# Two output units of mixer A in static weight slots, and a later attention and gated recurrence in the second layer

## The chip, the cores and the metric

The kernel runs on one core of a Trainium2 chip. TensorE (PE) does the matrix products, VectorE (DVE) and ScalarE (ACT) the elementwise work, SyncE (SP) issues most of the transfers and GpSimd (POOL) a few. The metric is the device time of one execution in microseconds (us), as the median of several runs.

## The reference

The reference is one inference step of a two-layer backbone on 128 context tokens and 256 latent tokens of width 1024. In each layer the normed tokens are scaled and shifted by a modulation, multiplied by one input projection, and go through four mixers side by side: A, a bidirectional RWKV-7 recurrence; B, a neighbourhood attention; C, a gated recurrence (HGRN2); D, a windowed attention with grouped heads. Their outputs, 256 columns each, are put side by side and multiplied by an output projection. Then a norm and a gate follow, the result is added to the residual, and a squared-ReLU MLP with 4096 hidden units does the same. In short:

```python
p = h @ w_in                                   # h = norm(x) * (1 + scale) + shift
y = concat([rwkv7(p), nat(p), hgrn2(p), swa(p)], -1) @ w_out
x = x + gate * rms(y)
h = rms(x) * (1 + scale2) + shift2
x = x + gate2 * rms(square(relu(h @ w1)) @ w2)
```

All is float32. Every float32 product is made of three products of a cheaper type, as the next section says.

## The kernel before

**Three products for one.** A float32 operand is split into a rounded big half and a remainder. A weight block of 128 x 1024, called a unit, arrives by a transfer in a slot `ws` (line 370), ACT casts its big half into `wh` (line 330), and DVE subtracts to make the remainder `wl` (line 318). The activations are split the same way into `hh` and `hl`. TensorE then adds wh x hh, wh x hl and wl x hh (line 333). An input unit is 24 matmuls of 384 columns, and a unit of the output projection is 18 matmuls of 512 columns.

**Slots.** The static slots live through the whole program: three `ws`, two `wh`, two `wl`. While the mixers run, all units use these. When a layer's mixers are done, `open_dense` opens further slots, `dws`, `dwh` and `dwl`, in memory that the mixers used. They are free only when the last reader of that memory is done. From then on `slot` (line 353) deals out static and dense slots in turns.

**Stages of a layer.** `rwkv_in` makes the first nine input units, which belong to mixer A. Then `merge` (line 1590) writes the four mixers interleaved: each has a clock that starts at an offset and runs at a rate, and the one whose clock is lowest is written next. The names ending in 1 are the second layer's: `ao1` is the offset of the neighbourhood attention, `ho1` that of the gated recurrence, `so1` that of the windowed attention, and `ul1` says how many steps the second half of mixer A stays behind the first. Mixer A's longest part is a chain: products, an inverse that goes through memory outside the core (transfers on SP at lines 957, 961, 973 and 977 with DVE work between them), then a set of 32 x 32 and 64 x 64 products, and `rwkv_post`, a norm on ACT and DVE that writes the two halves of mixer A's output into `hh` and `hl`.

**The end of a layer's mixing.** `wout_early` multiplies the six output units that belong to the mixers B, D and C. `wout` multiplies the two that belong to mixer A, units 0 and 1: unit 0 whole, unit 1 a 128-token tile at a time. Each tile then goes through `postnorm` (two squares with a sum on ACT, line 327; the root by a logarithm and an exponential; a scaled sum on DVE, lines 321 and 318, into the residual `x`) and `prenorm` (a square of `x`, the root, a scaling into `tmp`, line 324; eight transposes on TensorE, line 336; scale and shift; the split into `hh` and `hl`). The MLP begins with the first two units of w1, which wait for `hh`.

**What sets the order.** The program is written in the order that `merge` gives, but a scheduler then orders the instructions of each engine by a model of their durations. An engine runs its instructions in that order, and one that waits holds up all behind it. The model's price of a matmul pass is its columns by the clock and a constant gap.

Of the kernel before, what the change touches and what calls it, by code (L numbers as in the profile page):

```python
# [9 lines left out]

# [158 lines left out]
MIX = (5120, 12544, 15584)  # L169


P = {'hp': (0, 400), 'np': 3, 'we': 1, 'dp': [], 'ka': 0, 'pw': '', 'na': 2, 'nb': 2, 'pe': 'VAVA', 'xw': 4, 'wt': 4, 'xs': 2, 'mr': 2.5, 'ps': 7.4, 'po': 16, 'rw': (1.4, 1.4), 'ao': (80, 100), 'ar': (1.7, 1.4), 'so': (120, 120), 'sr': (1.4, 1.7), 'ho': (0, 0), 'hr': (0.8, 0.9), 'hl': (4, 4), 'lv': (2.0, 2.0), 'ul': (1, 1), 'rw0': 1.4, 'ao0': 80, 'ar0': 1.7, 'so0': 100, 'sr0': 1.4, 'ho0': 0, 'hr0': 0.9, 'hl0': 6, 'lv0': 4.0, 'ul0': 2, 'rw1': 1.4, 'ao1': 100, 'ar1': 1.7, 'so1': 120, 'sr1': 1.7, 'ho1': 0, 'hr1': 0.9, 'hl1': 4, 'lv1': 2.0, 'ul1': 3}
# [109 lines left out]
class Builder:  # L282
# [158 lines left out]
    def open_dense(self):  # L441
# [8 lines left out]
        for n, k, order in (("ws", self.xs, (0, 1)), ("wh", self.xw, (0, 1, 1)), ("wl", self.xw, (0, 1, 1))):  # L450
            q = self.pool("d" + n, k)
            self.wsets[n] = [((p[n], n), (q, "d" + n))[o] for o in order]
# [1179 lines left out]
    def dense_end(self, units, nxt, save, ahead=()):  # L1632
# [5 lines left out]
        for t in range(3):  # L1638
            for i, (src, y) in enumerate(units):
                self.rows_product(self.acc, *y, w[i], False, i == len(units) - 1, (t,))  # L1640
            self.postnorm(t, self.x[t], self.acc[t], self.gate)
            if save is not None:
                (self.nc.sync if save is self.io["y"] else self.nc.scalar).dma_start(save[t * 128:t * 128 + 128], self.x[t])
            if nxt is not None:
                self.prenorm(t, self.x[t], self.mods[nxt[0], nxt[1] + 1], self.mods[nxt[0], nxt[1]], self.h)
            yield len(units) * 1.3

# [4 lines left out]
    def mix(self, l, extra=()):  # L1652
# [15 lines left out]
        self.merge((0, p("rw"), self.rwkv(l), p("hp")), (p("ao"), p("ar"), attend(0), 0), (p("so"), p("sr"), attend(1), 0), (p("ho"), p("hr"), gated(), 0), *extra, then=self.wout_early(l))  # L1668
        self.open_dense()
# [16 lines left out]
    def wout(self, l):  # L1686
        s, y = self.wout_unit(l, 0)
        self.rows_product(self.acc, *y, self.unit(s), False, False)
        yield 3.9
        yield from self.dense_end([self.wout_unit(l, 1)], (l, 3), None, [self.io["w1"][l, n] for n in range(P["na"])])  # L1690
# [73 lines left out]
def program(layers=L, dbg=None):  # L1764
# [4 lines left out]
    for n, s in OUTS.items():  # L1769
        io[n] = nc.dram_tensor(n, s, F32, kind="ExternalOutput").ap()  # L1770
# [22 lines left out]
```

## Time and profile before

| What | us |
|---|---|
| median of 3 runs | 1402.37 |
| the runs | 1394.47, 1402.37, 1402.92 |
| profiled execution | 1390.85 |
| its span in the trace | 1389.1 |
| TensorE busy in the span | 1265.2 |

The profiled execution is 11.52 us shorter than the median. The span is cut into stages by the rows of the timeline: 0 to 60 is the start and the first modulation, 60 to 391 the first layer's mixers, 391 to 423 the end of its mixing, 423 to 742 its MLP, up to 752 the turn to the second layer, 752 to 1068 its mixers, 1068 to 1101 the end of its mixing, and 1101 to 1380 its MLP. A row of the timeline gives the start, the duration, the engine, the line, the operation and how many instructions it stands for; a bracket behind it gives the idle time of the engine just before it, and what ended that.

### The profile page before, as it was taken

Reading aid. Unit: us, or ns where it says so; the run is one execution under the profiler, and the core shown is the slowest. Engines: PE = TensorE matmul, PEld = TensorE weight load, DVE = VectorE, ACT = ScalarE, POOL = GpSimd, SP = SyncE. Lnnn points to the kernel's source line nnn. Section 1 sums busy time; section 2 is a strip of 40 time slices with the busy share of each in tenths; the row PEclk is TensorE's granted clock in tenths of the full one; section 3 lists DMA queues with packets and bytes.
Section 4 is the critical chain, followed back from the end, with each engine's and each line's share of the span. In section 5 each row is a group of like instructions: output and inputs, shape, how many; then the busy total and the mean of one; then the engine's idle time right before and its main releaser. Section 6 shows DMA issues by size and latency. Waiting matters only on the chain.

```text
span 1389.1 us, 20850 instructions
## 1 busy us (share of the span) xinstructions
PE 1265.2 (91%) x8174; PEld 1065.9 (77%) x8174; DVE 785.1 (57%) x1509; ACT 639.2 (46%) x1255; POOL 89.6 (6%) x165
## 2 busy tenths in 40 slices
PE   6899899899848999999997999899999499999997
PEld 2888788357738888878886888789776488999996
DVE  2598969644364444644544368987654633444442
ACT  4567533353254443534435578334544633333431
POOL 0000000000010212221000000100000000000000
PEclk8999899999986999999998999899999799999999
DMA  9332221761461888999852655136205454434411
GB/s 359 129 112 81 65 71 54 243 211 49 154 250 51 276 333 306 338 324 347 280 159 78 215 182 182 62 99 189 61 17 192 187 167 137 137 122 128 130 46 46
DMA packets 86899, 227.96 MB, mean 164 GB/s; under 512 B 24657, under 2 KB 27025, under 8 KB 86801
## 3 DMA queue, kind: packets, MB, share of 16 engines
q1 hardware_dynamic: 63040, 166.23, 36.8%
q0 software_dynamic: 12368, 44.60, 8.4%
q10 hardware_dynamic: 11392, 15.80, 3.6%
q8 instruction: 64, 1.05, 0.3%
q14 instruction: 35, 0.28, 0.1%
HBM read 205.33 MB, written 21.27 MB: 163 GB/s over the span
## 4 chain that ended last, share of the span: by engine, by line
PE 49%; DVE 9%; issue 6%; DMA 5%; ACT 4%; POOL 1%; SPq 0%; DVEq 0%; ACTq 0%; POOLq 0%
PE pd L333 24%; PE pr L333 12%; PE pm L333 11%; DVE mix L318 4%; DMA low<-wl 2%; ACT tmp L327 2%; DMA ws<-w 2%; ACT mix L327 1%; PE pm L336 1%; DVE tmp L321 1%; DVE wl L318 1%; DMA wl<-low 1%; DMA dws<-w 1%; ACT wh L330 1%; PE pd L336 1%
## 5 line engine op out<-in xcount | busy, mean ns | idle before, releaser
L333 PE MATMUL pd<-hh,wh 128*128 128x384 f32 (+2 forms) x640 | 221.6, 347 | 16.1 <-ACT hh L330 7.5
L333 PE MATMUL pd<-hh,wl 128*128 128x384 f32 (+2 forms) x640 | 221.3, 346 | 3.8 <-DVE wl L318 2.2
L333 PE MATMUL pd<-hl,wh 128*128 128x384 f32 (+2 forms) x640 | 218.6, 342 | 0.4 <-DVE hl L318 0.4
L330 ACT CAST wh<-ws 128x1024 fp32r<-128x1024 f32 x120 | 125.5, 1048 | 161.5 <-PE pd L333 67.8
L318 DVE TENSOR_TENSOR wl<-ws,wh 128x1024 fp32r<-128x1024 f32 x91 | 111.3, 1223 | 99.8 <-ACT wh L330 54.6
L318 DVE TENSOR_TENSOR mix<-mix 128x384 f32<-128x384 f32 (+19 forms) x288 | 134.6, 483 | 45.2 <-ACT mix L330 22.5
L333 PEld LDWEIGHTS pd<-hh,wh 128*128 128x128 f32 x640 | 124.4, 195 | 24.8 <-ACT hh L330 8.2
L333 PE MATMUL pd<-hh,dwh 128*128 128x384 f32 (+2 forms) x384 | 130.0, 341 | 8.4 <-ACT hh L330 6.7
L333 PEld LDWEIGHTS pd<-hh,wl 128*128 128x128 f32 x640 | 124.2, 194 | 10.4 <-issue 3.8
L333 PE MATMUL pd<-hl,dwh 128*128 128x384 f32 (+2 forms) x384 | 130.7, 341 | 0.7 <-DVE hl L318 0.6
L333 PE MATMUL pd<-hh,dwl 128*128 128x384 f32 (+2 forms) x384 | 130.2, 339 | 0.0
L333 PEld LDWEIGHTS pd<-hl,wh 128*128 128x128 f32 x640 | 124.6, 195 | 2.1 <-DVE hl L318 1.1
L327 ACT ACTIVATE mix<-mix 128x384 f32<-128x384 f32 (+4 forms) x188 | 106.9, 600 | 26.4 <-DVE mix L318 12.9
L333 PE MATMUL pr<-mix,mix 128*64 128x64 f32 (+3 forms) x1024 | 88.3, 238 | 9.3 <-DVE mix L318 6.3
L318 DVE TENSOR_TENSOR dwl<-ws,dwh 128x1024 fp32r<-128x1024 f32 x43 | 52.5, 1224 | 68.7 <-ACT dwh L330 67.2
L318 DVE TENSOR_TENSOR dwl<-dws,dwh 128x1024 fp32r<-128x1024 f32 x43 | 52.6, 1224 | 67.5 <-ACT dwh L330 67.5
L333 PEld LDWEIGHTS pr<-mix,mix 128*64 128x64 f32 (+3 forms) x1024 | 74.2, 149 | 20.3 <-issue 8.8
L333 PE MATMUL pm<-mix 128*32 128x32 f32 (+7 forms) x840 | 84.6, 271 | 2.1 <-DVE mix L318 1.3
L333 PEld LDWEIGHTS pd<-hh,dwh 128*128 128x128 f32 x384 | 75.5, 198 | 11.7 <-ACT hh L330 7.8
L333 PEld LDWEIGHTS pd<-hl,dwh 128*128 128x128 f32 x384 | 76.1, 198 | 2.9 <-DVE hl L318 1.5
L333 PE MATMUL pr<-dwh,f 128*128 128x512 f32 x240 | 77.2, 397 | 0.0
L330 ACT COPY mix<-pr 64x128 f32<-64x128 f32 (+7 forms) x136 | 42.2, 336 | 75.0 <-PE pr L333 45.4
(223 smaller groups left out, 2234.2 us busy)
## 6 DMA issues: line engine op xcount, KB each, us to landing
ws<-win SPq DMA_DIRECT2D x87, 512.0 KB, 4.5
ws<-w SPq DMA_DIRECT2D x64, 512.0 KB, 3.8
dws<-w SPq DMA_DIRECT2D x64, 512.0 KB, 5.2
wm<-modw POOLq DMA_DIRECT2D x56, 512.0 KB, 9.0
low<-wl POOLq DMA_DIRECT2D x29, 512.0 KB, 7.2
wl<-low SPq DMA_DIRECT2D x29, 512.0 KB, 3.8
ws<-modw SPq DMA_DIRECT2D x28, 512.0 KB, 4.8
ws<-wout SPq DMA_DIRECT2D x14, 512.0 KB, 4.6
```

The source lines that it names most:

```text
L318: (eng or self.nc.vector).tensor_tensor(out, a, b, op=op)
L321: self.nc.vector.scalar_tensor_tensor(out, a, s, b, op0=op0, op1=op1)
L327: self.nc.scalar.activation(out, a, fn, **kw)
L330: self.nc.scalar.copy(out, a)
L333: self.nc.tensor.matmul(out, l, r, start=start, stop=stop)
L336: self.nc.tensor.transpose(out, a, self.ident[:k, :k])
```

## The change

The static slots `wh` and `wl` become three each, and the dense slots `dwh` and `dwl` three each in place of four; `dws` is opened by another number (`xs`) and stays. The turns go dense, static, dense, static. At the end of `mix`, before the dense slots are opened, units 0 and 1 of the output projection are fetched and split in static slots (`self.last`), and `wout` uses them; the part of `dense_end` that norms one tile is a function of its own, `tile_end`. In the second layer the neighbourhood attention starts at clock 150 in place of 100, the gated recurrence at 40 in place of 0, and the second half of mixer A is two steps behind in place of three. The scheduler's gap for a matmul pass is set to 13 ns.

```diff
--- before.py
+++ after.py
@@ -7,6 +7,7 @@
 import concourse.tile as tile
 from concourse import mybir
 from concourse.bass_utils import run_bass_kernel_spmd
+from concourse.hw_specs import TRN2Spec
 
 F32 = mybir.dt.float32
 F32R = mybir.dt.float32r
@@ -166,10 +167,10 @@
 }
 
 
-MIX = (5120, 12544, 15584)
-
-
-P = {'hp': (0, 400), 'np': 3, 'we': 1, 'dp': [], 'ka': 0, 'pw': '', 'na': 2, 'nb': 2, 'pe': 'VAVA', 'xw': 4, 'wt': 4, 'xs': 2, 'mr': 2.5, 'ps': 7.4, 'po': 16, 'rw': (1.4, 1.4), 'ao': (80, 100), 'ar': (1.7, 1.4), 'so': (120, 120), 'sr': (1.4, 1.7), 'ho': (0, 0), 'hr': (0.8, 0.9), 'hl': (4, 4), 'lv': (2.0, 2.0), 'ul': (1, 1), 'rw0': 1.4, 'ao0': 80, 'ar0': 1.7, 'so0': 100, 'sr0': 1.4, 'ho0': 0, 'hr0': 0.9, 'hl0': 6, 'lv0': 4.0, 'ul0': 2, 'rw1': 1.4, 'ao1': 100, 'ar1': 1.7, 'so1': 120, 'sr1': 1.7, 'ho1': 0, 'hr1': 0.9, 'hl1': 4, 'lv1': 2.0, 'ul1': 3}
+MIX = (5120, 12544, 15488)
+
+
+P = {'hp': (0, 400), 'np': 3, 'we': 1, 'dp': [], 'ka': 0, 'pw': '', 'na': 2, 'nb': 2, 'pe': 'VAVA', 'xw': 3, 'wt': 4, 'xs': 2, 'mr': 2.5, 'ps': 7.4, 'po': 16, 'rw': (1.4, 1.4), 'ao': (80, 100), 'ar': (1.7, 1.4), 'so': (120, 120), 'sr': (1.4, 1.7), 'ho': (0, 0), 'hr': (0.8, 0.9), 'hl': (4, 4), 'lv': (2.0, 2.0), 'ul': (1, 1), 'rw0': 1.4, 'ao0': 80, 'ar0': 1.7, 'so0': 100, 'sr0': 1.4, 'ho0': 0, 'hr0': 0.9, 'hl0': 6, 'lv0': 4.0, 'ul0': 2, 'rw1': 1.4, 'ao1': 150, 'ar1': 1.7, 'so1': 120, 'sr1': 1.7, 'ho1': 40, 'hr1': 0.9, 'hl1': 4, 'lv1': 2.0, 'ul1': 2}
 
 
 def par(name, l):
@@ -447,7 +448,7 @@
         self.tmp = self.arena([a.tile([128, n], F32, name="tmp")], [n]).get
         self.wmod = self.pool("wm", 4)
         p = self.pools
-        for n, k, order in (("ws", self.xs, (0, 1)), ("wh", self.xw, (0, 1, 1)), ("wl", self.xw, (0, 1, 1))):
+        for n, k, order in (("ws", self.xs, (0, 1)), ("wh", self.xw, (1, 0)), ("wl", self.xw, (1, 0))):
             q = self.pool("d" + n, k)
             self.wsets[n] = [((p[n], n), (q, "d" + n))[o] for o in order]
 
@@ -1638,12 +1639,16 @@
         for t in range(3):
             for i, (src, y) in enumerate(units):
                 self.rows_product(self.acc, *y, w[i], False, i == len(units) - 1, (t,))
-            self.postnorm(t, self.x[t], self.acc[t], self.gate)
-            if save is not None:
-                (self.nc.sync if save is self.io["y"] else self.nc.scalar).dma_start(save[t * 128:t * 128 + 128], self.x[t])
-            if nxt is not None:
-                self.prenorm(t, self.x[t], self.mods[nxt[0], nxt[1] + 1], self.mods[nxt[0], nxt[1]], self.h)
+            self.tile_end(t, nxt, save)
             yield len(units) * 1.3
+
+    def tile_end(self, t, nxt, save):
+
+        self.postnorm(t, self.x[t], self.acc[t], self.gate)
+        if save is not None:
+            (self.nc.sync if save is self.io["y"] else self.nc.scalar).dma_start(save[t * 128:t * 128 + 128], self.x[t])
+        if nxt is not None:
+            self.prenorm(t, self.x[t], self.mods[nxt[0], nxt[1] + 1], self.mods[nxt[0], nxt[1]], self.h)
 
     def load_x(self):
         for t in range(3):
@@ -1666,6 +1671,7 @@
         self.run(self.rwkv_in(l, h))
         p = lambda n: par(n, l)
         self.merge((0, p("rw"), self.rwkv(l), p("hp")), (p("ao"), p("ar"), attend(0), 0), (p("so"), p("sr"), attend(1), 0), (p("ho"), p("hr"), gated(), 0), *extra, then=self.wout_early(l))
+        self.last = [self.unit(self.wout_unit(l, n)[0]) for n in (0, 1)]
         self.open_dense()
 
     def wout_unit(self, l, n):
@@ -1684,10 +1690,13 @@
             yield 3.9 * P["we"]
 
     def wout(self, l):
-        s, y = self.wout_unit(l, 0)
-        self.rows_product(self.acc, *y, self.unit(s), False, False)
-        yield 3.9
-        yield from self.dense_end([self.wout_unit(l, 1)], (l, 3), None, [self.io["w1"][l, n] for n in range(P["na"])])
+        units = [self.wout_unit(l, n) for n in (0, 1)]
+        self.prepare([self.io["w1"][l, n] for n in range(P["na"])])
+        self.rows_product(self.acc, *units[0][1], self.last[0], False, False)
+        for t in range(3):
+            self.rows_product(self.acc, *units[1][1], self.last[1], False, True, (t,))
+            self.tile_end(t, (l, 3), None)
+            yield 1.3
 
     def ffn(self, l, layers, halves):
         nc, io, h = self.nc, self.io, self.h
@@ -1768,11 +1777,12 @@
         io[n] = nc.dram_tensor(n, s, F32, kind="ExternalInput").ap()
     for n, s in OUTS.items():
         io[n] = nc.dram_tensor(n, s, F32, kind="ExternalOutput").ap()
+    TRN2Spec.PE_FULL_CLOCK_PASS_GAP_NS = 13.0
     with tile.TileContext(nc, schedule_with_timeline_sim=True) as tc:
         with ExitStack() as es:
             pool = lambda n, b, **kw: es.enter_context(tc.tile_pool(name=n, bufs=b, **kw))
             pools = {
-                "c1": pool("c1", 1), "ws": pool("ws", 3), "wh": pool("wh", 2), "wl": pool("wl", 2),
+                "c1": pool("c1", 1), "ws": pool("ws", 3), "wh": pool("wh", 3), "wl": pool("wl", 3),
                 "h": pool("h", 1), "prm": pool("prm", 1), "mt": pool("mt", 1),
                 "pm": pool("pm", 6 - P["np"], space=PSUM), "pr": pool("pr", P["np"], space=PSUM), "pd": pool("pd", 2, space=PSUM),
                 "dram": pool("dram", 2, space=DRAM), "spl": pool("spl", 1, space=DRAM),
```

The next rows are those of ACT at the end of the first layer's mixing. `mix_340` holds mixer A's values there, and the row with `eps` that reads `pr` is the logarithm in `rwkv_post`, once for each half of mixer A's output. Before:

```order
L327 ACTIVATE mix_340<-pr,eps 128x384
L327 ACTIVATE mix_340<-mix_340 128x384 x2
L327 ACTIVATE mix_340<-pr,eps 128x384
L330 CAST hh<-mix_340 128x384
L327 ACTIVATE mix_340<-mix_340 128x384
L519 DMA lora<-lora 128x768
L517 DMA prm<-prm 128x46
L330 CAST hh<-mix_340 128x384
L330 CAST dwh<-dws 128x1024 x2
L330 CAST dwh<-ws 128x1024 x2
L330 CAST wh<-dws 128x1024
L330 CAST dwh<-dws 128x1024
```

And now:

```order
L331 CAST dwh<-ws 128x1024 x2
L328 ACTIVATE mix_340<-mix_340 128x384
L331 CAST wh<-dws 128x1024
L328 ACTIVATE mix_340<-pr,eps 128x384
L328 ACTIVATE mix_340<-mix_340 128x384 x2
L331 CAST hh<-mix_340 128x384
L331 CAST dwh<-ws 128x1024
L328 ACTIVATE mix_340<-pr,eps 128x384
L520 DMA lora<-lora 128x768
L328 ACTIVATE mix_340<-mix_340 128x384
L518 DMA prm<-prm 128x46
L331 CAST hh<-mix_340 128x384
```

Four casts of the coming MLP's weights now stand ahead of the second half's logarithm, one of them from a dense slot; before, all casts of weights stood behind the last cast into `hh`.

The next rows are those of SP in the second layer's mixers, around the inverse in mixer A's chain. `inv` is its place outside the core, `wl<-low` is the remainder of an input unit that was split in advance, and `ws<-win` and `ws<-wout` are weight units. Before:

```order
L377 DMA wl<-low_4788 128x1024
L370 DMA ws<-win 128x1024
L377 DMA wl<-low_5046 128x1024
L370 DMA ws<-win 128x1024
L377 DMA wl<-low_4881 128x1024
L370 DMA ws<-wout 128x1024
L377 DMA wl<-low_5113 128x1024
L370 DMA ws<-wout 128x1024
L377 DMA wl<-low_5206 128x1024
L370 DMA ws<-wout 128x1024
L973 DMA inv<-mix_6234 96x1024
L977 DMA mix_6238<-inv 32x24x32 x4
```

And now:

```order
L958 DMA inv<-mix_6238 32x24x32 x4
L962 DMA mix_6234<-inv 96x1024
L378 DMA wl<-low_4598 128x1024
L371 DMA ws<-win 128x1024
L378 DMA wl<-low_4630 128x1024
L371 DMA ws<-win 128x1024
L378 DMA wl<-low_4721 128x1024
L371 DMA ws<-wout 128x1024
L974 DMA inv<-mix_6234 96x1024
L378 DMA wl<-low_4788 128x1024
L371 DMA ws<-wout 128x1024
L978 DMA mix_6238<-inv 32x24x32 x4
```

Between the first read of the inverse (line 961) and the last, six pairs of weight transfers stood before, of which the last five are shown, and four stand now; one of these is now between the write and the last read.

The last rows are those of DVE at the end of the second layer's mixing, where the three tiles are normed; the three tiles of `x` are `x_8968` to `x_8970` before. Before:

```order
L318 TENSOR_TENSOR wl<-dws,wh 128x1024
L318 TENSOR_TENSOR dwl<-ws,dwh 128x1024
L321 SCALAR_TENSOR_TENSOR tmp<-pd,tmp,gate 128x512 x2
L321 SCALAR_TENSOR_TENSOR tmp<-pm,tmp,gate 128x512 x2
L321 SCALAR_TENSOR_TENSOR tmp<-pr,tmp,gate 128x512
L321 SCALAR_TENSOR_TENSOR tmp<-pm,tmp,gate 128x512
L318 TENSOR_TENSOR x_8968<-x_8968,tmp 128x512 x2
L318 TENSOR_TENSOR x_8969<-x_8969,tmp 128x512 x2
L318 TENSOR_TENSOR x_8970<-x_8970,tmp 128x512 x2
L324 TENSOR_SCALAR tmp<-x_8968,tmp 128x512
```

And now, where they are `x_9033` to `x_9035`:

```order
L322 SCALAR_TENSOR_TENSOR tmp<-pd,tmp,gate 128x512 x2
L319 TENSOR_TENSOR x_9033<-x_9033,tmp 128x512
L319 TENSOR_TENSOR tmp<-tmp 128x1
L319 TENSOR_TENSOR x_9033<-x_9033,tmp 128x512
L319 TENSOR_TENSOR wl<-dws,wh 128x1024
L322 SCALAR_TENSOR_TENSOR tmp<-pm,tmp,gate 128x512 x2
L322 SCALAR_TENSOR_TENSOR tmp<-pr,tmp,gate 128x512
L322 SCALAR_TENSOR_TENSOR tmp<-pm,tmp,gate 128x512
L325 TENSOR_SCALAR tmp<-x_9033,tmp 128x512
```

The first tile's residual is now ready before the other tiles' sums; before, it came behind the sums of all three. In the first layer the change goes the other way: there the first tile was ready first, and now the sums of all three tiles come ahead of it.

## Rows read from the trace of the kernel before

**Rows 1.** The page: busy time, share of the span, instructions of each engine.

```profile
PE 1265.2 (91%) x8174; PEld 1065.9 (77%) x8174; DVE 785.1 (57%) x1509; ACT 639.2 (46%) x1255; POOL 89.6 (6%) x165
```

**Rows 2.** Windows by stage: length, busy us of each engine, granted clock, DMA share, GB/s.

```profile
60.00:391.00 331.00, 301.84 (x2368) 243.44 (x2366) 228.61 (x513) 157.11 (x357) 13.81 (x33) 0.94 0.37 112
391.00:423.00 32.00, 14.21 (x52) 11.18 (x52) 25.08 (x43) 22.12 (x48) 3.51 (x5) 0.72 0.80 291
752.00:1068.00 316.00, 298.39 (x2401) 257.43 (x2401) 208.16 (x486) 163.54 (x372) 13.11 (x31) 0.96 0.40 126
1068.00:1101.00 33.00, 13.43 (x53) 10.95 (x52) 25.21 (x40) 21.31 (x49) 2.90 (x4) 0.74 0.66 255
1101.00:1380.00 279.00, 278.05 (x1439) 249.29 (x1440) 114.93 (x148) 100.25 (x150) 3.40 (x5) 0.99 0.36 112
```

**Rows 3.** Windows, the steady part of the first layer's MLP.

```profile
460.00:700.00 240.00, 236.88 (x1282) 196.66 (x1280) 118.99 (x156) 104.90 (x139) 47.35 (x72) 1.00 0.89 316
```

**Rows 4.** Waits of PE: line, releaser, us in total, times, the longest.

```profile
PE pd L336 <- DVE tmp L324: 21.9, 2, 13.8
...
PE pd L333 <- ACT dwh L330: 10.0, 2, 7.1
```

**Rows 5.** Timeline of PE, the end of the first layer's mixing.

```profile
389.66 0.91 PE L333 MATMUL pr<-mix,lora 128*128 128x384 f32 x2
397.65 1.22 PE L333 MATMUL pd<-dwh,hh 128*128 128x512 f32 x2 [7.08 <-ACT dwh L330]
...
403.68 0.62 PE L333 MATMUL pd<-wh,hh 128*128 128x512 f32 x2
...
407.54 0.39 PE L333 MATMUL pr<-wh,hl 128*128 128x512 f32 x1
416.06 1.97 PE L336 MATMUL pd<-cst,tmp 128*128 128x128 f32 x8 [8.13 <-DVE tmp L324]
...
423.11 0.80 PE L333 MATMUL pd<-hh,dwh 128*128 128x256 f32 x2 [3.07 <-ACT hh L330]
```

**Rows 6.** Timeline of ACT, the same stretch.

```profile
393.43 0.51 ACT L330 CAST hh<-mix 128x384 fp32r<-128x384 f32 x1 [2.44 <-DVE mix L318]
396.55 1.04 ACT L330 CAST dwh<-dws 128x1024 fp32r<-128x1024 f32 x1 [2.61 <-DMA dws<-wout]
```

**Rows 7.** Timeline of DVE, the same stretch.

```profile
394.44 0.55 DVE L318 TENSOR_TENSOR hl<-mix,hh 128x384 fp32r<-128x384 f32 x1
```

**Rows 8.** Timeline of PE, the end of the second layer's mixing.

```profile
1070.98 1.22 PE L333 MATMUL pd<-dwh,hh 128*128 128x512 f32 x2 [2.93 <-ACT dwh L330]
...
1076.61 0.63 PE L333 MATMUL pd<-wh,hh 128*128 128x512 f32 x2
...
1094.64 1.97 PE L336 MATMUL pd<-cst,tmp 128*128 128x128 f32 x8 [13.77 <-DVE tmp L324]
...
1101.04 0.67 PE L333 MATMUL pd<-hh,dwh 128*128 128x256 f32 x2 [2.92 <-ACT hh L330]
```

**Rows 9.** Windows of 2 us, while unit 0 of the second layer runs.

```profile
1072.00:1074.00 2.00, 2.00 (x6) 1.60 (x5) 1.79 (x3) 0.90 (x2) 1.37 (x2) 0.52 1.03 406
1074.00:1076.00 2.00, 2.00 (x10) 1.60 (x9) 1.53 (x2) 2.00 (x3) 0.00 (x0) 1.00 0.99 365
```

**Rows 10.** Timeline of SP, mixer A's inverse in the second layer (write, then read back).

```profile
913.66 5.95 SPq L957 DMA_DIRECT2D inv<-mix  x4
921.49 0.32 SPq L961 DMA_DIRECT2D mix<-inv  x1
...
957.12 0.38 SPq L973 DMA_DIRECT2D inv<-mix  x1
962.49 2.12 SPq L977 DMA_DIRECT2D mix<-inv  x4
```

**Rows 11.** Timeline of PE in the second layer's mixers.

```profile
879.90 1.65 PE L333 MATMUL pr<-mix,mix 64*128 64x128 f32 x6 [2.86 <-DVE mix L318]
...
923.76 0.34 PE L333 MATMUL pd<-hl,wh 128*128 128x384 f32 x1
...
925.34 0.34 PE L333 MATMUL pd<-hl,wh 128*128 128x384 f32 x1
...
966.47 1.60 PE L333 MATMUL pr<-mix,mix 32*32 32x32 f32 x48
```

## The prediction

> **What bounds the kernel now.** I read the shares of busy time first: TensorE is busy 1265.2 us of a span of 1389.1, DVE only 785.1 [rows 1]. So an edit can gain only where TensorE stands idle, about 124 us in all. The windows by stage say where that is [rows 2]. In the MLPs there is almost nothing to win: 278.05 of 279 us are busy in the second, 236.88 of 240 in the steady part of the first [rows 2, 3]. In the mixers TensorE idles 331 - 301.84 = 29.2 us in the first layer and 316 - 298.39 = 17.6 us in the second, in many small pieces. Dense idle time lies at the two ends of the mixing: 32 - 14.21 = 17.8 us and 33 - 13.43 = 19.6 us [rows 2]. The list of waits names two releasers there: the scaled residual that the transposes need, 21.9 us in two waits, and the big half of a unit in a dense slot, 10.0 us in two [rows 4]. The change is aimed at the second and also reorders the first. The reader should see in [rows 5, 8] that each end is a line of four pieces: wait for unit 0's weights, two units of products, wait for the norm, transposes and the wait for `hh`.
>
> **First layer's end.** Before, the products wait until 397.65, for 7.08 us, for the cast of unit 0 from a dense slot, which starts at 396.55 after 2.61 us without work on ACT, for its transfer [rows 5, 6]. With units 0 and 1 in static slots, what comes last is mixer A's output itself: its second half is cast at 393.43 and its remainder ends at 394.44 + 0.55 = 395.0 [rows 6, 7]. But the order of ACT has new casts ahead of that. Two at 1.04 us are 2.1, and the one that reads a dense slot can wait for its transfer, between 0 and the 2.61 us seen [rows 6]; I take 0.8, because that memory is now given free earlier. So the remainder ends at 395.0 + 2.9 = 397.9. Unit 0 needs only the first half and runs before that. Unit 1 takes what a unit took at the full clock, 403.68 to 407.54 + 0.39 = 4.25 us, and ends at 402.1 in place of 407.9: -5.8 us. Bounds: -8.7 without any delay by the casts, -4.0 with the whole 2.61.
>
> Then the norm. This layer's order becomes what the second layer's was, all three tiles' sums ahead of the first scaling. The second layer's wait for it is 13.77 us, this one's 8.13 [rows 5, 8]. One cast of 1.04 us fewer stands in it, so 13.77 - 1.04 - 8.13 = +4.6 us. From the transposes to the MLP it was 423.11 - 416.06 = 7.05 us here and 1101.04 - 1094.64 = 6.40 there: -0.65. Together the first end gives -5.8 + 4.6 - 0.65 = **-1.9 us** (-4.8 to 0).
>
> **Second layer's end.** The attention now ends after mixer A, and 132 of the 144 products of the output projection stand in one piece behind it. Mixer A's norm, the gate's transfers that SP issues and the fetches of units 0 and 1 have six units of 4.25 us as cover, 25 us, where a wait at this place was 2.93 us [rows 8]; I cost them at nothing. If that cover were gone, the 2.93 us would be back. The wait goes: -2.93. Unit 0 ran at half clock (0.52 in its window, 1.00 in the next [rows 9]) and took 1076.61 - 1070.98 = 5.63 us; behind a full queue it takes 4.25: -1.4. The order of the norm becomes what the first layer's was: 8.13 in place of 13.77, -5.6, and 7.05 in place of 6.40 behind it, +0.65. Sum **-9.3 us** (-11 to -4, the latter if the order gains only half of its 5.6 and the wait keeps 2.9).
>
> **What the second layer's mixers give back.** The later attention and gated recurrence take work away from where it covered mixer A's chain. (a) The inverse lasts from the write at 913.66 to the read-back that ends at 962.49 + 2.12 us, and TensorE takes up its result at 966.47 with no wait named [rows 10, 11]. Between its reads SP now has four pairs of weights in place of six. An input unit is 24 matmuls with starts (925.34 - 923.76) / 9 = 0.176 us apart, 4.2 us [rows 11], so two are 8.4 us of cover. One weight pair also stands between SP's write and its last read; if its slot is not free it holds the chain up, and TensorE can at worst wait these 8.4 us. At best nothing is lost, for DVE, which does the inverse, has less other work ahead. I take +3, nearest to the row of the longest wait for DVE in these mixers, 2.86 us [rows 11]. (b) The attention's softmax at the end has only 12 products beside it: 0 to +5, by the same row for one or two waits, taken +2. (c) No output products stand in the last part of mixer A's chain any more, the attention's stand there: 0, up to +5. Sum **+5** (0 to +18).
>
> **The rest.** A third static pair lets the weights be split one unit further ahead; dense pairs go from four to three, so six stay. Both are covered by the busy MLPs [rows 2, 3]: 0. If the cover were gone, it would be in the first MLP, where the transfers are at 0.89 [rows 3]; its idle is 3.1 us, and I bound it by that again, +3. Memory of the mixers shrinks by 96 elements: 0. Nothing of weight moves on POOL's queue.
>
> The gap of 13 ns is not work on the chip; it only orders the instructions. [...] I take 0, -4 to +6, a fifth of the first layer's idle 29.2 us on the bad side. [...]
>
> **Sum.** -1.9 - 9.3 + 5 = -6.2 us. Against the profiled 1390.85 that is 1384.6. That execution lies 11.5 us below the median of 1402.37, so the forecast in the same terms as the median is **1396 us**.
>
> **Rivals.** *Both ends' gains are kept* (0.27). Nothing is given back, and the deeper static slots and earlier chain take half of the mixers' idle 17.6 us too: -11.2 - 8.8 = -20, 1382 us. For it: DVE's inverse has less beside it. Against: the waits of the mixers are mostly DVE's, which lose no work.
>
> *The chain is uncovered* (0.17, the slower side). Mixer A's inverse and the attention's softmax leave TensorE without work. All of (a) to (c), 8.4 + 5 + 5 = 18.4 us, and two units at half clock behind the waits, 2 x 1.4 = 2.8, make 21 - 11.2 = +10: 1412 us. It decides when the give-back passes 11.2 us. For it: four pairs in place of six on SP. Against: TensorE's work in this layer is the same, and its last 30 us now need no mixer A. The half clock is what the trace shows behind a wait, 0.52 after 2.93 us [rows 8, 9]. [...]
>
> *The new order costs as much in the first layer* (0.11). That layer's offsets stay, so only the gap and the slots move its work; at the bad end of +6 the sum is 0: 1402 us, as if the change did nothing. [...]
>
> **Numbers.** Forecast 0.45, with its own range 1388 to 1404. A range of 1380 to 1412 leaves out the lower half of the first rival and the upper half of the second, about 0.2. A measurement of this kernel can tell some 1% from no change, 14 us: below 1388.3 or above 1416.4. Faster: 0.23 of the first rival and 0.06 of the forecast, 0.29. Slower: 0.09 of the second rival, 0.03 for costs not seen, 0.12. Same: 0.59.
>
> **What would show it.** In the changed profile the two waits for `dwh` should be gone, and the products of unit 1 in the first layer end some 6 us nearer to mixer A's last product. The two waits for the scaled residual should have changed places: about 12.7 us in the first layer, about 8 in the second. TensorE's idle in the second layer's mixers should be some 5 us above 17.6, with a wait ahead of the first 32 x 32 products. If those products come without a wait, the first rival holds; if they wait over 8 us, or the attention's end shows several waits, the second. The MLPs should take the same time; if they don't, a term that I set at zero was wrong.

## The result

The changed kernel is slower: a median of 1407.57 us against 1396.38 in twenty runs each, ratio 1.0112 with a 95% interval of 1.0088 to 1.0136. The forecast was 1396 us against 1402.37, a little faster, a ratio of 0.9955. (1407.57 lies between 1380 and 1412 only in number: the median of three runs that the forecast starts from stood 6 us above that of twenty.) The profiled execution has a span of 1407.2 us, 18.1 more than before. The comparisons leave disturbed executions out.

One thing ahead of the prediction stands the wrong way round: the number that goes from four to three opens the landing slots `dws`; `dwh` and `dwl` stay four. So the split pairs go from six to seven in all, where the prediction has "so six stay", and the landing slots from seven to six.

TensorE does the same 8174 matmuls. Its busy line after the change answers to the one before [rows 1]; busy time is 16.5 us longer for the same work.

```profile
PE 1281.7 (91%) x8174; PEld 1076.5 (76%) x8174; DVE 782.0 (56%) x1509; ACT 641.4 (46%) x1258; POOL 89.8 (6%) x165
```

The windows of the changed kernel, cut where its stages end: first layer's mixers to the last output product, its norm, its MLP, then the same of the second layer. The columns are those of [rows 2].

```profile
60.00:407.10 347.10, 312.54 (x2391) 250.56 (x2389) 235.46 (x525) 162.30 (x362) 16.42 (x36) 0.93 0.40 125
407.10:426.60 19.50, 3.72 (x17) 3.32 (x17) 14.44 (x29) 12.90 (x38) 0.00 (x0) 0.61 0.20 66
426.60:760.60 334.00, 314.39 (x1658) 262.13 (x1658) 155.37 (x215) 143.83 (x217) 49.82 (x76) 0.98 0.74 261
760.60:1100.70 340.10, 319.31 (x2437) 275.37 (x2437) 222.03 (x506) 177.50 (x397) 17.04 (x37) 0.92 0.43 136
1100.70:1115.50 14.80, 3.98 (x18) 3.17 (x17) 13.78 (x28) 11.64 (x31) 0.00 (x0) 0.63 0.27 94
1115.50:1398.30 282.80, 282.18 (x1440) 254.04 (x1441) 113.83 (x146) 99.14 (x149) 3.40 (x5) 0.97 0.36 110
```

And the kernel before, cut in the same way:

```profile
60.00:407.90 347.90, 312.09 (x2404) 251.49 (x2402) 238.82 (x528) 166.49 (x375) 16.75 (x37) 0.94 0.39 123
407.90:423.10 15.20, 3.96 (x17) 3.13 (x16) 14.87 (x29) 12.84 (x32) 0.57 (x1) 0.63 0.66 241
423.10:752.20 329.10, 314.51 (x1658) 266.30 (x1658) 158.28 (x219) 144.19 (x221) 49.94 (x77) 0.96 0.74 261
752.20:1080.90 328.70, 308.33 (x2437) 265.14 (x2437) 218.00 (x498) 171.47 (x384) 16.01 (x35) 0.95 0.41 132
1080.90:1101.00 20.10, 3.48 (x16) 3.24 (x16) 15.35 (x28) 13.18 (x37) 0.00 (x0) 0.66 0.60 243
1101.00:1380.20 279.20, 278.25 (x1440) 249.45 (x1441) 114.93 (x148) 100.25 (x150) 3.40 (x5) 0.99 0.36 112
```

The reader is to see four things in this pair of executions. The second layer's mixers take 11.4 us longer with the same 2437 matmuls: TensorE idles 20.8 us in place of 20.4, but is busy 11.0 us more, at a clock of 0.92 in place of 0.95 (a granted clock of 0.50, half clock below, is the lowest that either profile shows). Of its busy time 53.7 us lie at half clock after and 30.1 before; with half of that taken off, 292.5 and 293.3 us are left, so the work is the same. The first MLP takes 4.9 us longer, all idle (19.6 against 14.6). The two norms have changed places, +4.3 and -5.3 us. And the second MLP takes 3.6 us longer, at a clock of 0.97 in place of 0.99. How far the clock's part holds beyond this pair, the section on the experiments says. The waits and the timeline of TensorE at the two ends, after the change:

```profile
PE pd L337 <- DVE tmp L325: 20.0, 2, 13.1
```

```profile
395.04 1.65 PE L334 MATMUL pr<-mix,cst 128*128 128x384 f32 x2 [2.46 <-ACT mix L328]
396.47 1.49 PE L334 MATMUL pr<-mix,lora 128*128 128x384 f32 x2
...
402.68 0.73 PE L334 MATMUL pd<-wh,hh 128*128 128x512 f32 x2 [0.60 <-ACT hh L331]
...
406.67 0.39 PE L334 MATMUL pr<-wh,hl 128*128 128x512 f32 x1
420.15 1.97 PE L337 MATMUL pd<-cst,tmp 128*128 128x128 f32 x8 [13.10 <-DVE tmp L325]
...
426.56 0.58 PE L334 MATMUL pd<-hh,wh 128*128 128x256 f32 x1 [2.73 <-ACT hh L331]
...
974.84 1.66 PE L334 MATMUL pr<-mix,mix 32*32 32x32 f32 x48
...
1107.64 1.97 PE L337 MATMUL pd<-cst,tmp 128*128 128x128 f32 x8 [6.93 <-DVE tmp L325]
...
1115.47 0.58 PE L334 MATMUL pd<-hh,dwh 128*128 128x256 f32 x1 [2.39 <-ACT hh L331]
```

The waits for `dwh` are gone (7.08 and 2.93 us in [rows 5, 8]), and the residual's waits are 13.10 and 6.93 us where they were 8.13 and 13.77. But the first layer's last output product ends at 407.06, not 402.1, because mixer A's own last product (`pr<-mix,lora`) ends at 398.0 and not at 390.6. ACT shows why mixer A's second half comes later than the 393.43 of [rows 6]:

```profile
390.08 1.04 ACT L331 CAST wh<-dws 128x1024 fp32r<-128x1024 f32 x1 [1.05 <-DMA dws<-w]
...
397.54 1.05 ACT L331 CAST dwh<-ws 128x1024 fp32r<-128x1024 f32 x1 [2.11 <-DMA ws<-w]
...
402.12 0.51 ACT L331 CAST hh<-mix 128x384 fp32r<-128x384 f32 x1 [2.49 <-DVE mix L319]
```

### The profile page after: what moved, and what is told of

It is laid out like the page before. It is cut to its first block, busy times and chain, and to the rows that moved or that the text cites. A ratio compares the mean times of both kernels' runs of the same rounds, so it can differ in the third digit from the quotient of the medians.

```text
span 1407.2 us, 20835 instructions
## 1 busy us (share of the span) xinstructions
PE 1281.7 (91%) x8174; PEld 1076.5 (76%) x8174; DVE 782.0 (56%) x1509; ACT 641.4 (46%) x1258; POOL 89.8 (6%) x165
## 3 DMA queue, kind: packets, MB, share of 16 engines
q8 instruction: 64, 1.05, 0.3%
## 5 line engine op out<-in xcount | busy, mean ns | idle before, releaser
L334 PE MATMUL pd<-hh,wh 128*128 128x384 f32 (+2 forms) x752 | 262.4, 350 | 12.6 <-ACT hh L331 8.9
L334 PE MATMUL pd<-hl,wh 128*128 128x384 f32 (+2 forms) x752 | 259.9, 346 | 1.7 <-DVE hl L319 1.7
L319 DVE TENSOR_TENSOR mix<-mix 128x384 f32<-128x384 f32 (+17 forms) x280 | 127.6, 471 | 33.9 <-ACT mix L331 22.5
L331 ACT CAST dwh<-ws 128x1024 fp32r<-128x1024 f32 x62 | 64.9, 1049 | 143.2 <-DMA ws<-w 99.9
L328 ACT ACTIVATE mix<-mix 128x384 f32<-128x384 f32 (+3 forms) x182 | 104.0, 599 | 47.2 <-DVE mix L319 23.0
L319 DVE TENSOR_TENSOR wl<-dws,wh 128x1024 fp32r<-128x1024 f32 x62 | 75.8, 1223 | 86.0 <-ACT wh L331 75.1
L331 ACT CAST wh<-dws 128x1024 fp32r<-128x1024 f32 x62 | 65.0, 1048 | 109.8 <-PE pd L334 72.1
L331 ACT COPY mix<-pr 64x128 f32<-64x128 f32 (+7 forms) x136 | 42.1, 337 | 87.3 <-PE pr L334 60.5
L334 PE MATMUL pm<-mix 64*32 64x32 f32 (+7 forms) x700 | 75.6, 279 | 4.6 <-DVE mix L319 2.6
L334 PEld LDWEIGHTS pm<-mix 128*128 128x128 f32 (+5 forms) x700 | 57.7, 162 | 17.4 <-issue 6.2
L334 PE MATMUL pr<-mix 128*64 128x64 f32 (+2 forms) x832 | 66.2, 235 | 3.9 <-ACT mix L331 3.8
```

Of the source, the lines that this page charges most:

```text
L319: (eng or self.nc.vector).tensor_tensor(out, a, b, op=op)
L328: self.nc.scalar.activation(out, a, fn, **kw)
L331: self.nc.scalar.copy(out, a)
L334: self.nc.tensor.matmul(out, l, r, start=start, stop=stop)
```

## The experiments

All ratios are to the kernel before, run beside each, with 95% intervals. The lengths are of one profiled execution each. "Half" is the time of a stretch at half clock (twice its length times one less its granted clock), TensorE's idle time included. The last column is of all executions: the mean of the span times one less the granted clock, and in brackets that of the kernel before beside it. It holds idle time at half clock too, 17 us of it in either profile of the last section. The edits are shown cut down to what matters.

| Run | Ratio | Mixers 1, us / half | MLP 1, us / idle | Mixers 2, us / half | Norms 1, 2, us | Lost to the clock, us |
|---|---|---|---|---|---|---|
| before | 1 | 347.9 / 44 | 329.1 / 14.6 | 328.7 / 32 | 15.2, 20.1 | 79 |
| changed | 1.0112 (1.0088 to 1.0136) | 347.1 / 48 | 334.0 / 19.6 | 340.1 / 57 | 19.5, 14.8 | 81 |
| gap alone | 1.0094 (1.0063 to 1.0125) | 345.5 / 44 | 328.6 / 15.1 | 346.0 / 67 | 15.4, 22.0 | 84 (79) |
| offsets alone | 0.9923 (0.9899 to 0.9947) | 341.5 / 34 | 325.5 / 15.8 | 328.1 / 28 | 15.1, 14.8 | 68 (79) |
| slots and early fetch | 1.0105 (1.0065 to 1.0144) | 358.9 / 82 | 321.7 / 8.0 | 339.3 / 53 | 20.8, 19.3 | 104 (79) |
| the same and offsets | 1.0001 (0.9972 to 1.0030) | 354.8 / 72 | 321.4 / 6.8 | 333.0 / 39 | 20.8, 14.8 | 91 (79) |
| slots only | 1.0029 (1.0001 to 1.0056) | 360.2 / 85 | 314.4 / 6.1 | 334.0 / 44 | 19.8, 19.5 | 91 (77) |
| early fetch only | 0.9988 (0.9958 to 1.0018) | 332.8 / 34 | 328.6 / 14.6 | 332.3 / 53 | 22.8, 22.3 | 78 (77) |
| offsets and early fetch | 0.9999 (0.9975 to 1.0024) | 336.3 / 38 | 324.6 / 13.9 | 333.6 / 34 | 22.8, 19.1 | 70 (77) |

**What one profile can say of the clock.** In these nine profiles TensorE's busy time, less half of what of it lies at half clock, is 1207 to 1212 us. So the work is the same in all, a us of busy time at half clock costs half a us, and a span is that work, this loss and the idle time. But the loss changes from execution to execution. The kernel before lost 65 to 91 us in 34 executions on one chip, and an execution that lost 1 us more was 0.73 us longer (103 executions on five chips). So the last column corrects what single profiles seem to say. The pair of profiles in the last section puts 15 of its 18 us on the clock (89 us lost against 74); over all executions it is 81 against 79 (77 to 82 on the five chips), so on average a lower clock is not what makes the changed kernel slower. The gap alone loses 6 us more to it and is 13 slower. The slots with the early fetch lose 26 us more and are 15 slower; the offsets lose 10 less and are 11 faster. Where the rest of the gap's and the changed kernel's loss lies is not shown: equal idle times at unequal clocks, such as 20.8 and 20.4 us above, do not exclude added waits. The second MLP, not in the table, takes 278 to 285 us, with 3 to 5 or 14 to 17 us at half clock, and both of these come in one order.

**The three parts apart.** Theory 1 put the loss on the offsets, theory 2 on the gap, theory 3 on the slots.

```diff
+    TRN2Spec.PE_FULL_CLOCK_PASS_GAP_NS = 13.0
```

> The kernel before, with nothing but the scheduler's gap of 13 ns. Theory 1 (the later attention and recurrence of the second layer cost the time): the gap does nothing, ratio 1.000 within 0.004, and the second layer's mixing from the first input unit to its last product stays at 329 us. Theory 2 (the gap's new orders cost it): most of the 1.1% is here, ratio 1.006 to 1.012, with the end of the first layer's chain some 7 us later (390.6 to 398) and more waits for ACT in the first MLP. Theory 3 (the slots cost it): 1.000. My forecast took 0 with -4 to +6 us.

Measured 1.0094, about 13 us, as theory 2 says; but the place was wrong. In the profile the first layer did not get longer. The second layer's mixers did, by 17.3 us, with 67 us at half clock; by the last column the clock explains less than half of the loss in the mean.

```diff
-'ao1': 100, 'ho1': 0, 'ul1': 3
+'ao1': 150, 'ho1': 40, 'ul1': 2
```

> The kernel before, with nothing but the second layer's offsets and lag (attention 150, gated recurrence 40, lag 2). Theory 1: slower by 8 to 15 us, ratio 1.006 to 1.011, all of it between the second layer's first input unit and its last product (329 us before, 340 in the changed kernel). Theories 2 and 3: within 4 us of no change; by the give-back of my forecast, +5 us less the shorter norm of 5.6 us, about 0.

Measured 0.9923, about 11 us faster: theory 1 falls. These are its two rows for the second layer's mixers and norm:

```profile
742.10:1070.20 328.10, 303.84 (x2437) 261.11 (x2437) 218.05 (x500) 175.07 (x393) 16.50 (x37) 0.96 0.44 144
1070.20:1085.00 14.80, 3.99 (x18) 3.18 (x17) 13.78 (x28) 11.64 (x31) 0.00 (x0) 0.63 0.20 63
```

The mixers are as long as before and the norm is 5.3 us shorter; that gain is the offsets' and not the early fetch's. This profile does not place the 11 us, though: its second MLP took 5.3 us more (284.5, clock 0.97), and it is shorter by 10 us ahead of the second layer, where both kernels run the same instructions in the same order.

```diff
-    TRN2Spec.PE_FULL_CLOCK_PASS_GAP_NS = 13.0
-'ao1': 150, 'ho1': 40, 'ul1': 2
+'ao1': 100, 'ho1': 0, 'ul1': 3
```

> The changed kernel without the gap and with the old offsets: three static and three dense slot pairs, units 0 and 1 of the output projection fetched early. Theory 1: faster by the waits at the two ends, 2 + 4 to 9 us, ratio 0.993 to 0.997. Theory 3: slower, 1.005 to 1.011, with the MLPs 4 to 5 us longer each (329 and 288 us before) since dense and static slots take turns one by one. Theory 2: faster as in theory 1.

Measured 1.0105: theory 3's size, but not its place. The first MLP was 7.4 us shorter; the first layer's mixers were 11.0 us longer, at 0.89 of the clock, and the second layer's 10.6.

```diff
-    TRN2Spec.PE_FULL_CLOCK_PASS_GAP_NS = 13.0
```

> The changed kernel without the gap of 13 ns alone. Theory 1: still slower, ratio 1.006 to 1.012, the second layer's mixing at 338 to 341 us. Theory 2: the loss is gone, 0.990 to 1.000, and the first layer's chain ends near 390.6 us again. Theory 3: 1.005 to 1.011 with longer MLPs.

Measured 1.0001: without the gap the loss is gone, as theory 2 says. The first layer's chain does not end near 390.6, though, but at 405.9. So two parts lose about 1% each and the third gains 0.8%: 0.94 + 1.05 - 0.77 = 1.22 against 1.12 measured.

**The slots and the early fetch apart.**

```diff
+"wh": pool("wh", 3), "wl": pool("wl", 3)
+'xw': 3
+("wh", self.xw, (1, 0)), ("wl", self.xw, (1, 0))
```

> The kernel before with the slots alone (three static pairs of big half and remainder, three dense landing slots in place of four, turns one by one), units 0 and 1 of the output projection as before, no gap, old offsets. Theory A (the third static pair lets the wide input units run ahead, and leaves a stretch of small products of the first layer alone, in which the clock falls): as slow as the slots with the early fetch, ratio 1.007 to 1.013, with more than 70 us at half clock in the first layer's mixers (44 before, 82 there). Theory B (the early fetch of units 0 and 1 and the casts that it puts ahead of mixer A's norm cost it): 0.998 to 1.002, about 44 us at half clock.

```diff
+        self.last = [self.unit(self.wout_unit(l, n)[0]) for n in (0, 1)]
         self.open_dense()
```

> The kernel before with the early fetch of units 0 and 1 and the new wout alone, two static pairs as before. Theory A: no loss, 0.992 to 1.000; the wait for the dense slot's cast of 7.1 and 2.9 us goes or is paid elsewhere. Theory B: slower, 1.005 to 1.012.

Slots 1.0029, early fetch 0.9988: neither theory A nor B, since the two together cost more than the sum. Theory A's half-clock time is there, 85 us; but the first MLP, 14.7 us shorter, pays for most of it.

> The kernel before with the second layer's new offsets (ratio 0.9923) and the early fetch of units 0 and 1, two static pairs, no gap. Theory A: as the offsets alone or better by the wait for the dense slot's cast in the first layer, up to 7 us: 0.987 to 0.993. Theory B: worse than the offsets alone, 0.997 to 1.004.

Measured 0.9999, theory B's side. The offsets' gain does not stand beside the early fetch: the second norm is 19.1 us again, and the first, 22.8, is 7.6 us longer than before, as with the early fetch alone.

**Where the slots lose.** The rows of the slots with early fetch, in the first layer's mixers: windows of 10 us, then TensorE's timeline.

```profile
180.00:190.00 10.00, 8.61 (x69) 6.74 (x68) 9.75 (x20) 2.60 (x6) 1.02 (x3) 0.80 0.38 112
190.00:200.00 10.00, 10.00 (x55) 8.82 (x55) 2.30 (x5) 2.32 (x14) 0.63 (x2) 0.50 0.06 15
200.00:210.00 10.00, 10.00 (x89) 7.74 (x89) 2.35 (x5) 1.74 (x5) 0.00 (x0) 0.50 0.11 20
210.00:220.00 10.00, 10.00 (x58) 9.41 (x59) 5.80 (x11) 2.66 (x6) 1.73 (x4) 0.66 0.26 61
```

```profile
186.65 0.74 PE L334 MATMUL pm<-mix 64*64 64x64 f32 x12 [0.82 <-DVE mix L322]
...
193.76 2.24 PE L334 MATMUL pr<-mix,mix 64*128 64x128 f32 x12
...
213.30 0.67 PE L334 MATMUL pd<-hh,wh 128*128 128x384 f32 x1
```

Some 27 us hold small products alone but for three matmuls of an input unit. The clock falls to 0.50 behind two short waits (0.57 and 0.82 us), and stays there with TensorE busy 10.00 of 10 us, until input units stand there again: 30.7 us, and as much in the run with the offsets, which has this order too. The gap alone has a like stretch in its second layer:

```profile
890.00:900.00 10.00, 6.32 (x48) 5.53 (x47) 9.81 (x22) 2.57 (x6) 0.00 (x0) 0.77 0.00 0
900.00:910.00 10.00, 10.00 (x88) 8.16 (x88) 7.76 (x14) 1.69 (x2) 0.43 (x1) 0.50 0.01 2
910.00:920.00 10.00, 9.76 (x100) 8.16 (x101) 8.31 (x15) 5.38 (x11) 1.22 (x3) 0.71 0.06 16
```

```profile
894.77 2.40 PE L334 MATMUL pm<-mix,mix 128*128 128x128 f32 x12 [3.68 <-DVE mix L319]
...
910.51 5.15 PE L334 MATMUL pm<-mix 128*32 128x32 f32 x62
915.59 1.35 PE L334 MATMUL pr<-mix,mix 64*128 64x128 f32 x12
```

There a longer wait, 3.68 us, stands ahead of the fall, and the clock is back at 915.8 among small products, without an input unit. So in this profile it came back without wide work.

Whether waits start the low clock is not shown; none stands in the 20 us at 0.50 from 190 to 210 of the run with the slots and the early fetch.

**Wide work beside the small products.** Two idle matmuls of 384 columns ahead of each group of small products, first written into the program:

```diff
                 ps = self.pr()
+                for _ in range(self.fill):
+                    self.mm(ps[:, 0:T], self.h[0][:, 0, 0:128], self.h[0][:, 0])
```

> The slots with the early fetch (ratio 1.0105), and in the first layer's mixer A two idle matmuls of 384 columns more ahead of each of the 16 groups of its small products, whose results are overwritten: 32 matmuls, 32 x 0.176 = 5.6 us of work added at the full clock, nothing else changed but the order that the scheduler then finds. Theory A (the clock falls where small products stand alone): the half-clock time of the first layer's mixers falls from 82 to 30 to 55 us, and the mixing gets 8 to 20 us shorter by that in spite of 5.6 us more work, ratio 0.998 to 1.006. Theory C (the time is lost to waits or to work, the clock only follows): 1.013 to 1.018, the added work on top.

Measured 0.9977 (0.9947 to 1.0007): work added and 1.3% gained. But the scheduler had laid out the whole order anew, and input units stand between the small products there. The other four speak for the order and against the idle work:

> The gap of 13 ns alone (ratio 1.0094) and, in the second layer's mixer A, the two idle matmuls of 384 columns ahead of each of 16 groups of small products, 5.6 us of added work. Theory A (the new orders leave small products alone in the second layer's mixers, 67 us at half clock there against 30 before): the half-clock time there falls to 25 to 45 us and the ratio to 0.997 to 1.004. Theory C (the orders of the gap cost waits or work): 1.013 to 1.016.

Measured 1.0098 (1.0064 to 1.0132), second layer's mixers 350.7 us with 54 at half clock.

> The changed kernel (ratio 1.0112) with the idle matmuls in both layers' mixer A, 11.3 us of added work. Theory A: its mixers lose 48 and 56 us at half clock, fewer than the slots alone in the first layer; 30 to 40 in each by this, so 13 to 17 us less for 11.3 us more work and the rest kept: 1.000 to 1.010. Theory C: 1.018 to 1.022.

Measured 1.0457 (1.0410 to 1.0504): second layer's mixers 387.0 us, 106 at half clock, 42.1 idle.

> The changed kernel without the gap (ratio 1.0001), with the idle matmuls in both layers. Theory A: the first layer gains as with the slots alone, -12 us net, the second, with 38 us at half clock, nothing net: 0.989 to 0.997, faster than both kernels. Theory C: 1.007 to 1.010.

Measured 1.0256 (1.0217 to 1.0294), second layer's mixers 372.0 us with 72 at half clock and 43.7 idle.

> The kernel before with the idle matmuls in the first layer alone, 5.6 us of added work, a control. Theory A: its first layer has 44 us at half clock, some 17 of it where small products stand, so at most 8 us come back for 5.6 us paid: 0.996 to 1.004, far from the 18 us that the slots gained by it. Theory D (idle wide matmuls help any order of this kernel alike): 0.985 to 0.990.

Measured 1.0079 (1.0045 to 1.0113), 11 us. All four are misses for theory A; the changed kernel got 48 us slower by its re-laid order and the added work together.

So the idle matmuls were put into the finished order, behind a group's first matmul, where the rest of the group overwrites what they leave:

```diff
+            if n in groups:
+                for e in range(each):
+                    new.append(copy.replace(i, name=..., outs=[ou], ins=[hh, lw], sync_info=None))
```

> The slots with the early fetch (ratio 1.0105, 82 us at half clock in the first layer's mixers), and two idle matmuls of 384 columns behind the first matmul of each of the first layer's 16 groups of small products, put into the finished order: every other instruction stands where it stood. Added work 32 x 0.176 = 5.6 us at the full clock. Theory A (small products alone let the clock fall): half-clock time there 35 to 60 us, the mixing 5 to 18 us shorter less up to 5.6, ratio 0.998 to 1.007. Theory E (the clock follows from the order's waits, whatever the products are): 75 to 85 us, ratio 1.013 to 1.018.

Measured 1.0252 (1.0202 to 1.0302), 85 us at half clock: a miss for theory A, even above theory E. What is paid was mis-sized, though, here and in the next runs. The price of 0.176 us is that of a stream; busy time, less half of its half-clock part, is 1219.1 us in place of 1208.3, so these 32 cost 10.8 us, 0.34 each. In the next three runs it is 11.3 us for 32, and 26.7 and 20.3 for 64; in eights, 15.9 for 64.

> The gap alone (ratio 1.0094, 67 us at half clock in the second layer's mixers), with the idle matmuls in the second layer's 16 groups and the order kept. Theory A: half-clock time there 35 to 55 us, ratio 1.001 to 1.008. Theory E: 62 to 70 us, 1.012 to 1.016.

Measured 1.0105 (1.0054 to 1.0156). The profile has 72 us at half clock, as theory E has it, but its clock of 0.938 is the lowest of six; their mean is 0.948 against 0.940 of the gap alone. With 11.3 us paid, some 10 came back (2 to 18 by the two intervals), which is theory A's side.

> The changed kernel (ratio 1.0112, 48 and 56 us at half clock in the two layers' mixers) with the idle matmuls in both layers, 11.3 us of added work, order kept. Theory A: 30 to 40 us in each, ratio 1.005 to 1.012, since about as much comes back as is paid. Theory E: 1.018 to 1.022.

Measured 1.0251 (1.0203 to 1.0300): above both by their price, but 26.7 us, 0.019, were paid. Half-clock time was 38 and 51 us in the profile, with a clock of 0.946; over six executions the clock is 0.942, as without the idle work.

> The kernel before with the idle matmuls in both layers, order kept, the control: its groups of small products have fewer bare stretches (44 and 30 us at half clock, most of it behind waits of 2 to 3 us). Theory A: little comes back, ratio 1.003 to 1.009. Theory E: 1.007 to 1.010, all of the 11.3 us paid.

Measured 1.0192 (1.0133 to 1.0252): above both, with 79 us at half clock in the second layer in place of 32. Of the 27 us, 20.3 are the added work.

> The slots with the early fetch (ratio 1.0105), order kept, eight idle matmuls of 384 columns behind the first matmul of each of the eight groups that lie in the first layer's bare stretch (186 to 213 us): 64 x 0.176 = 11.3 us of work at the full clock. Theory A (wide work next to small products holds the clock, if there is enough of it): half-clock time between 180 and 235 us under 14 us (31 before), 8 or more us come back, ratio 1.003 to 1.014. Theory E (the clock falls by something else in that stretch): 30 us or more at half clock there, and up to 22 us longer at it, ratio 1.019 to 1.028.

Measured 1.0194 (1.0139 to 1.0249), as theory E has it; but the clock did what theory A says, in this one stretch:

```profile
190.00:200.00 10.00, 10.00 (x36) 8.67 (x36) 2.50 (x4) 1.46 (x3) 0.82 (x2) 0.50 0.04 15
200.00:210.00 10.00, 10.00 (x61) 8.19 (x61) 1.67 (x3) 1.33 (x12) 0.00 (x0) 0.86 0.07 15
210.00:220.00 10.00, 10.00 (x93) 7.86 (x91) 1.67 (x3) 1.73 (x5) 0.00 (x0) 1.00 0.09 15
```

With two idle matmuls the same place was at 0.50 until 230:

```profile
200.00:210.00 10.00, 10.00 (x44) 7.61 (x43) 1.12 (x2) 2.33 (x14) 0.00 (x0) 0.50 0.06 15
210.00:220.00 10.00, 10.00 (x73) 6.94 (x72) 1.67 (x3) 1.75 (x5) 0.00 (x0) 0.50 0.00 0
220.00:230.00 10.00, 10.00 (x53) 6.87 (x52) 2.03 (x4) 0.00 (x0) 0.00 (x0) 0.50 0.12 21
```

In this stretch 17 us are at half clock, against 31 without idle work and 41 with two a group, in one profile each. So in that profile, with eight a group, the clock was back at 1.00 among small products. It does not pay here.

**The version the runs pointed to.**

> The changed kernel without the gap, with two idle matmuls of 384 columns ahead of each group of small products in the first layer, so that the scheduler finds the first layer's order of the run with slots and wide fill (350 us to the last product, 34 of them at half clock, and an MLP of 317 us), and the second layer's of the run with slots and offsets (333 us, norm 14.8). If a time belongs to an order, whatever brought it about: span near 60 + 350 + 20 + 317 + 333 + 15 + 290 = 1385, ratio 0.986 to 0.993, faster than both kernels. If the times are the idle matmuls' or the offsets' own: 0.998 to 1.004.

Measured 0.9975 (0.9935 to 1.0016), a miss. Its first layer has the order of the run with slots and wide fill, but in the profile not its time: 361.1 us with 61 at half clock, where that had 349.8 with 34. The next rows are that pair, the run with slots and wide fill first:

```profile
60.00:409.80 349.80, 312.98 (x2422) 249.70 (x2420) 233.19 (x524) 160.07 (x360) 16.45 (x36) 0.95 0.39 125
```

```profile
60.00:421.10 361.10, 323.95 (x2419) 257.98 (x2417) 233.16 (x524) 160.13 (x360) 16.41 (x36) 0.91 0.38 121
```

The same instructions in the same order differ by 11 us between two profiled executions (on two chips), by the clock: idle time is 36.8 and 37.1 us. Over twelve executions each, the two kernels lose 66 and 69 us to the clock, so the pair is chance. Before and offsets alone, alike up to the second layer, differ by 6.4 us in the first layer's mixers. Idle time in the first MLP is steady in one order (8.0, 6.8, 6.8 and 7.2 us in four runs with the slots' order, 19.6 and 19.1 in two with the changed kernel's); time at half clock is not. The best version measured is the offsets alone: 0.8% faster than before, and so about 1.9% faster than the changed kernel.

## Why the prediction was wrong

- **The first layer's end, -1.9 us.** Both halves of the mechanism came: the wait for `dwh` went, and the norm's wait became 13.10 us where 12.7 was worked out. Counted from mixer A's last product, unit 1 ended 8.3 us nearer (9.1 us behind it in place of 17.4), where 6 were forecast. But that product ended 7.4 us later, at 398.0, and the sum had left it where it was; so unit 1's end moved by -0.9 and not by -5.8. I counted two of the four casts that the new order shows, all behind that product, and gave them 0.8 us of waiting for transfers; two of the four waited 1.05 and 2.11, and TensorE waited 2.46 for ACT ahead of mixer A's last products, 1.26 before. How much of the 7.4 us that makes, and how much the clock of this execution, is not shown. The MLP began 3.45 us later in place of 1.9 earlier.
- **The second layer's end, -9.3 us.** The wait of 2.93 went, the units behind it ran at a clock of 1.00, the wait for the residual fell to 6.93 (8.13 predicted), but what follows it took 7.8 us in place of 7.05. The norm as a whole gained 5.3. The offsets alone give all of this, with units 0 and 1 fetched as before.
- **The give-back, +5 us.** As waits it did not come: the first 32 x 32 products at 974.84 follow without one, and the idle time is 20.8 us against 20.4. The offsets alone measure -0.8%, 11 us, where -9.3 + 5 makes -4.3: nothing was given back.
- **"The rest", 0.** This is the step that failed. "The gap of 13 ns is not work on the chip; it only orders the instructions", at 0, -4 to +6: measured alone, it costs 0.94% or 13 us, outside my bounds. No run shows the 0: the trace has 512-column matmuls 0.227 us apart [rows 5], not how much of that is a gap, and the run with the gap alone has +13 us. The slots ("Both are covered by the busy MLPs") had 0 too: the first MLP did gain, 7 to 15 us, but the mixers of the first layer lost 7 to 12 us, and with the early fetch the kernel lost 1.05%. Both edits re-lay the whole order, and I priced them as if only waits could come of that. For the slots the runs show the loss: 26 us more go to the clock in the mean of all executions, and all three profiles with the slots have the stretch of small products in the first layer's mixers, 31 to 34 us at half clock. My sum had no term for that; the clock had one at the two ends and in a rival. For the gap the clock gives less than half of the 13 us, and the rest stays open. The MLPs did not take the same time (+4.9 and +3.6 us in the pair of profiles), the sign that the prediction names for a term wrongly set at zero.
- **The rivals.** "The chain is uncovered" gave 1412 us and the right side, by the wrong mechanism: no wait of 8 us came. The case with the gap named the first layer, +6; it was the second layer's mixers (+17.3 alone) and, beside the slots, the first MLP: its idle time is 6.8 us without the gap and 19.6 with it (19.1 in the run that keeps this order). Whether the price of 13 ns brings the scheduler's picture nearer to the chip is not shown; the kernel got slower by it.

**What stays open.** By what the gap's order is slower, beyond 6 us of clock and the idle time in the MLP beside the slots, is not shown; the kept profiles differ too much in clock. Whether a property of the small products keeps the clock low, and which (columns, rows of the array, or type), was not tried. Whether the two short waits or the small products start the fall is not told apart. Why the offsets' gain vanishes beside the early fetch was not tried; the longer norms are all that the profile shows of it.

## What to carry to other kernels

Where a scheduler lays out the order, an edit that looks local, or is only a price in its model, can cost as much as any other: price the whole order, and cost such an edit with bounds of a per cent on both sides. In a stretch where TensorE is busy, read the granted clock beside the busy time; the same count of matmuls in a longer busy time is a loss that no list of waits shows (here 8174 matmuls in 1281.7 us in place of 1265.2). But read that clock over many executions before you call it the cause: here one pair of profiles put 15 us on it and the mean of all executions 2. Take edits of one commit apart before believing their sum: here two losses of 1% hid a gain of 0.8%.

## What the runs showed of the hardware

With the slots and the early fetch, TensorE stayed at half clock for 30.7 us in the first layer's mixers, of which 20 were busy 10.00 of 10 us with products of 32 to 128 columns but for three matmuls; eight matmuls of 384 columns among each group brought it back to 1.00 there, two did not, in one profiled execution each. One program lost 65 to 91 us to the clock in 34 executions on one chip, with granted clocks of 0.935 to 0.953; and the same order of instructions took 349.8 and 361.1 us in two executions, with the clock at 0.95 and 0.91. A matmul of 384 columns, 0.176 us in a stream, cost 0.32 to 0.42 us in a pair among small products.
